# The last 256 tokens leave transposed and scaled on their way out of PSUM, and the end's products use both banks of a PSUM tile

## Chip, cores and metric

The kernel runs on one core of one Trainium2 chip. The metric is the device time of one execution in microseconds, given as the median of repeated runs. The two outermost times of the kernel before are 0.17% apart.

## The reference, cut to what matters

One layer of a streaming encoder is applied to 640 tokens (512 of a new prompt, 8 x 16 of running streams), with 1024 features each. Only its end is touched by the change: the down-projection of the ConvGLU, the residual, and the last RMSNorm.

```
D_MODEL = 1024
D_FF = ((8 * D_MODEL // 3 + 255) // 256) * 256        # 2816

def rms_norm(x, g):
    xf = x.astype(jnp.float32)
    y = xf * lax.rsqrt(jnp.mean(xf * xf, axis=-1, keepdims=True) + RMS_EPS)
    return (y * g.astype(jnp.float32)).astype(x.dtype)

def hybrid_layer(x, ...):
    ...
    out = h + (jax.nn.gelu(c) * b) @ p['w_down']
    return out, s_re, s_im, new_k, new_v, new_conv

y_prompt = rms_norm(hp, g_final)
y_sample = rms_norm(hs, g_final)
```

## The kernel before

Everything is kept transposed: features on the 128 partitions (8 blocks `h_[0..7]` of 128 features), the 640 tokens along the free axis. Every product with a weight is made of three products of split values (high x high, high x low, low x high), all through the helper `mm` (L115).

The order on each engine is written by hand. The program is a list of segments; `tick()` runs before each and issues what `later(n, fn)` has put down for that place. Each engine then works through its own queue in order, and waits on counters that the other engines advance.

The 2816 inner features go through the ConvGLU in six parts. The last part has `pn` = 4 blocks, and its down-projection is the end of the program. It goes over the tokens in two stretches, `segs = ((0, 384), (384, 640))`: first the eight output blocks i = 0..7 for tokens 0 to 383 (stretch A), then again the eight blocks for tokens 384 to 639 (stretch B). In the text "product i" is one such block: 4 inner blocks x 3 = 12 matmuls, issued by `fin_mm` in four calls, one per tick.

PSUM has two pools. `bigps()` gives a tile [128, 2, 512] of float32, which is two banks, from a ring of two such tiles (names `pb`). `smps(tag)` gives single banks `sX`, `sP`, `sS`, `sT`, one of each. `fin_mm` takes a fresh `bigps()` tile for each product and uses its bank 0 alone:

```
if k == 0:
    cur[i] = bigps()
ps = cur[i][:, 0, 0:e - a]
```

When a product is complete, `fin_evac` adds it to the residual (VectorE, L1505), squares it (ScalarE, L1509, L1511 or L1514), and adds the square to a running sum (VectorE, L1515). After product 7, `fin_stat` makes the RMSNorm scales: `s0` sums the squares over the partitions by matmuls with ones and takes the root (L1539 to L1541), `s1` refines the reciprocal on VectorE down to `ys`, one scale per token with tokens on partitions (L1544 to L1548), `s2` spreads it over all partitions by matmuls with the identity. For stretch A ScalarE copies that to `RS` (L1555), and the outputs follow during stretch B, two per product, by `fin_out`: one VectorE instruction h x gain x scale (L1524) and one DMA of SyncE (L1525). For stretch B the same eight VectorE instructions stand at the very end, reading the scale from PSUM, and their DMAs alternate between the queues of SyncE and ScalarE. The output `o_y` is (8, 128, 640), and the host turns it round.

Of the kernel before, what the change touches and what calls it, by code (L numbers as in the profile page):

```python
# [11 lines left out]
AF = mybir.ActivationFunctionType  # L12
OP = mybir.AluOpType
# [3 lines left out]
T, NS, TS = 640, 8, 16  # L17
HT = 320
D, DFF = 1024, 2816
KD, KF = 8, 22  # L20
# [5 lines left out]
SEG_A = 384  # L26
# [13 lines left out]
C_GM, C_GF, C_GO, C_CW, C_CB = 0, 8, 16, 24, 90  # L40
# [3 lines left out]
def body(nc, tc, d, ctx):  # L44
# [8 lines left out]
    V, A, G, PE, S = nc.vector, nc.scalar, nc.gpsimd, nc.tensor, nc.sync  # L53
# [3 lines left out]
    def nm(s):  # L57
        uid[0] += 1
        return f"{s}{uid[0]}"

    def ht(dt=F32, w=T):
        return heap.tile([128, w], dt, tag="T", name=nm("h"))

    def bigps():
        return psb.tile([128, 2, 512], F32, tag="big", name=nm("pb"))

    def smps(tag):
        return pss.tile([128, 512], F32, tag=tag, name=nm(tag))
# [4 lines left out]
    def vcol(c):  # L73
        return vec[:, c:c + 1]


    ident = const.tile([128, 128], F32, name="ident")
# [3 lines left out]
    RS = const.tile([128, T], F32, name="RS")  # L81
    rst = const.tile([128, 32], F32, name="rst")
# [31 lines left out]
    def mm(ps, lhs, rhs, start, stop):  # L114
        PE.matmul(ps, lhs, rhs, start=start, stop=stop)  # L115
# [19 lines left out]
    def later(n, fn):  # L135
        events.setdefault(clock[0] + n, []).append(fn)
# [3 lines left out]
    def tick():  # L140

        while clock[0] in events:
            for fn in events.pop(clock[0]):
                fn()
        if side[0] is not None:
            side[1] += side[2]
            while side[1] >= 1.0 and side[0] is not None:
                side[1] -= 1.0
                if next(side[0], "end") == "end":
                    side[0] = None  # L150
        clock[0] += 1
# [899 lines left out]
    n = 0  # L1051
# [32 lines left out]
    for i in range(8):  # L1084
        if i in (2, 4, 5, 6):
            p = pair()
            a = att[(2, 4, 5, 6).index(i)]
# [46 lines left out]
    a_t, c_t = tmp[:, 0:NA], tmp[:, NA:NA + L]  # L1134
# [112 lines left out]
    segs = []  # L1247
# [129 lines left out]
    def block(key, n):  # L1377
        c = 128 * (n % 4)
        return [t[:, c:c + 128] for t in ops[key][n // 4]]
# [45 lines left out]
    for p, nf in enumerate(PARTS):  # L1425
        for j in range(nf):
            f = f0 + j
            q = len(segs)
# [22 lines left out]
            e = q + 2 * (f == 0)  # L1451
# [7 lines left out]
            if prev is not None:  # L1459
# [8 lines left out]
                for o in range(per):  # L1468
                    i = j * per + o
# [11 lines left out]
    q = len(segs)  # L1481
# [16 lines left out]
    segs = ((0, SEG_A), (SEG_A, T))  # L1498
    accs = [ht(), ht()]
    last = [ht(), ht()]  # L1500

    def fin_evac(sg, i, ps):
        a, b = segs[sg]
        hs = h_[i][:, a:b]
        V.tensor_tensor(hs, ps, hs, op=OP.add)  # L1505

        def sq():
            if i == 0:
                A.activation(accs[sg][:, 0:b - a], hs, AF.Square)  # L1509
            elif i == 7:  # L1510
                A.activation(last[sg][:, 0:b - a], hs, AF.Square)  # L1511
            else:
                q = ht()
                A.activation(q[:, 0:b - a], hs, AF.Square)  # L1514
                V.tensor_tensor(accs[sg][:, 0:b - a], accs[sg][:, 0:b - a], q[:, 0:b - a], op=OP.add)  # L1515
        (later if sg == 0 else now)(1, sq)

    def now(n, fn):
        fn()

    def fin_out(sg, i, rs):
        a, b = segs[sg]
        o = ht()
        V.scalar_tensor_tensor(o[:, 0:b - a], h_[i][:, a:b], vcol(C_GO + i), rs, op0=OP.mult, op1=OP.mult)  # L1524
        (S if i % 2 == 0 or sg == 0 else nc.scalar).dma_start(d["o_y"][i, :, a:b], o[:, 0:b - a])  # L1525

    def fin_stat(sg):

        a, e = segs[sg]
        n, t0 = (e - a) // 128, a // 128  # L1530
        p1 = smps("sS")
        v, r, w = rst[:, 24:24 + n], rst[:, 16:16 + n], rst[:, 20:20 + n]
        y, ys = rst[:, 13:13 + n], rst[:, 27:27 + n]

        def s0():
            for t in range(n):
                for i, x in enumerate((accs[sg], last[sg])):
                    mm(p1[:, 2 * t:2 * t + 2], x[:, t * 128:t * 128 + 128], ones[:, 0:2], i == 0, i == 1)
            V.tensor_tensor(w, p1[:, 0:2 * n:2], rst[:, 8 + t0:8 + t0 + n], op=OP.mult)  # L1539
            A.activation(r, w, AF.Sqrt, scale=1.0 / D, bias=eps)  # L1540
            V.tensor_scalar(v, w, -0.5 / D, -0.5 * EPS, op0=OP.mult, op1=OP.add)  # L1541

        def s1():
            V.reciprocal(y, r)  # L1544
            V.tensor_tensor(r, y, y, op=OP.mult)
            V.tensor_tensor(r, r, v, op=OP.mult)
            V.scalar_tensor_tensor(y, r, 1.5, y, op0=OP.add, op1=OP.mult)
            V.tensor_tensor(ys, y, rst[:, t0:t0 + n], op=OP.mult)  # L1548

        def s2():  # L1550
            p2 = smps("sT" if sg == 0 else "sX")
            for t in range(n):
                mm(p2[:, t * 128:t * 128 + 128], rst[:, 27 + t:28 + t].to_broadcast([128, 128]), ident, True, True)
            if sg == 0:
                A.activation(RS[:, a:e], p2[:, 0:e - a], AF.Copy)  # L1555
            return p2
        return s0, s1, s2

    cur = {}

    def fin_mm(sg, b):
        i, k = divmod(b, pn)
        if k == 0:
            cur[i] = bigps()
        a, e = segs[sg]
        ps = cur[i][:, 0, 0:e - a]
        key, o = tail[i]
        hi, lo = block(key, o * pn + k)
        ch, cl = cs[pf + k]
        mm(ps, hi, ch[:, a:e], k == 0, False)  # L1570
        mm(ps, hi, cl[:, a:e], False, False)
        mm(ps, lo, ch[:, a:e], False, k == pn - 1)
        if k == pn - 1:
            later(0, lambda: fin_evac(sg, i, ps))
            if i == 7:
                st = fin_stat(sg)
                if sg == 0:
                    for j, f in enumerate(st):
                        later(4 + 2 * j, f)
                    for j in range(8):  # L1580
                        later(10 + 2 * j, lambda j=j: fin_out(0, j, RS[:, a:e]))
                else:
                    fin.extend(st)
    fin = []
    for b in range(8 * pn):
        tick()
        fin_mm(0, b)
    later(0, lambda: nc.scalar.dma_start(d["o_c"], oc))
    for b in range(8 * pn):
        tick()  # L1590
        fin_mm(1, b)
    tick()
    fin[0]()
    fin[1]()
    rs = fin[2]()[:, 0:T - SEG_A]
    for i in range(8):
        fin_out(1, i, rs)
    while events:
        tick()
    xctx2.close()  # L1600
# [84 lines left out]
    return o  # L1685


OUTS = {"o_y": (8, 128, T), "o_k": (4, 128, T), "o_v": (5, 128, 512), "o_s": (128, 2, 16, 9), "o_c": (128, KF, 18)}


def build(arrays):
    nc = bacc.Bacc("TRN2", target_bir_lowering=False, num_devices=1)
    d = {}
    for name, a in arrays.items():
        d[name] = nc.dram_tensor("in_" + name, a.shape, mybir.dt.from_np(a.dtype), kind="ExternalInput").ap()
    for name, s in OUTS.items():
        d[name] = nc.dram_tensor(name, s, F32, kind="ExternalOutput").ap()
    with tile.TileContext(nc) as tc, ExitStack() as ctx:
        body(nc, tc, d, ctx)
    return nc  # L1700


def unpack(r):
    y = r["o_y"].reshape(D, T).T
    k = r["o_k"].reshape(512, T).T
    v = r["o_v"].reshape(T, 512)
    s = r["o_s"].reshape(2, 64, 2, 16, 9).transpose(2, 4, 3, 0, 1).reshape(2, 9, 32, 64)
    cv = r["o_c"].transpose(2, 1, 0).reshape(18, DFF)

    def c(a, *shape):  # L1710
        return np.ascontiguousarray(a.reshape(shape))
    return (c(y[:512], 1, 512, D), c(y[512:], 8, 16, D),
            c(s[0, 0], 1, 1, 32, 64), c(s[1, 0], 1, 1, 32, 64),
            c(k[:512], 1, 1, 512, 8, 64), c(v[:512], 1, 1, 512, 8, 64),
            c(cv[:2], 1, 1, 2, DFF),
            c(s[0, 1:], 1, 8, 32, 64), c(s[1, 1:], 1, 8, 32, 64),
            c(k[512:], 1, 8, 16, 8, 64), c(v[512:], 1, 8, 16, 8, 64),
            c(cv[2:], 1, 8, 2, DFF))
# [7 lines left out]
```

## Time and profile before

| | |
|---|---|
| median of 3 runs | 951.29 us (951.09 to 952.75) |
| profiled execution, its own time | 955.98 us |
| its span, first to last instruction | 953.9 us |
| TensorE busy / VectorE / ScalarE / GpSimd | 97% / 66% / 46% / 14% of the span |
| mean granted TensorE clock | 0.985 of full speed |

The profile shows one execution, on one core. "PE" is TensorE's matmul, "PEld" its weight load, "DVE" VectorE, "ACT" ScalarE, "SP" SyncE; "PEq" or "SPq" is the instruction queue of an engine, from which DMAs are issued. A row of the timeline gives start, duration, engine, line, operation, what it writes and reads, and in brackets how long the engine had been idle and what ended that. Two matmuls in a row overlap in the records, so the distance of their starts is what one costs.

### The profile page before, as it was taken

To read this page: it belongs to the slowest core of one execution; us is meant where nothing else is said; L and a number is where in the kernel's file an instruction comes from. 1 tells how busy PE (TensorE), PEld (TensorE's weight loads), DVE (VectorE), ACT (ScalarE), POOL (GpSimd) and SP (SyncE) were. 2 spreads that over 40 slices of the span, in tenths; PEclk is the share of its full clock that TensorE was granted. 3 is DMA by queue.
4 is the path that set the end of the run, shared out by engine and by line. 5 is a ranking of instruction groups with operands and counts; after the bars stand their busy time and mean duration, and the time that the engine had idled before them with its cause. 6 is when DMAs were issued, how large, how long until landed. Compare 5 with 4: busy or idle time off the path is not lost.

```text
span 953.9 us, 16515 instructions
## 1 busy us (share of the span) xinstructions
PE 923.4 (97%) x6534; PEld 875.8 (92%) x6534; DVE 628.0 (66%) x1261; ACT 442.1 (46%) x689; POOL 133.4 (14%) x228
## 2 busy tenths in 40 slices
PE   8999999999999999999998989999999999999995
PEld 8978999977777799999998989999999999999994
DVE  6783996474665543566777877766766676666545
ACT  6244113343333364433667445545455545555441
POOL 0120403200000000000003212212122211222100
PEclk9999999999999999999999999999999999999998
DMA  6744329666647522234538778889878888899833
GB/s 223 198 137 125 133 68 110 216 199 215 169 129 230 159 81 67 72 105 158 136 84 178 156 165 188 206 186 200 196 178 187 201 191 180 197 191 192 189 57 110
DMA packets 62428, 151.76 MB, mean 159 GB/s; under 512 B 20944, under 2 KB 24208, under 8 KB 62352
## 3 DMA queue, kind: packets, MB, share of 16 engines
q1 hardware_dynamic: 45392, 95.90, 33.3%
q0 software_dynamic: 16096, 54.03, 29.9%
q8 instruction: 51, 0.84, 0.4%
q10 hardware_dynamic: 864, 0.78, 0.2%
q14 instruction: 25, 0.20, 0.1%
HBM read 114.56 MB, written 8.21 MB: 129 GB/s over the span
## 4 chain that ended last, share of the span: by engine, by line
PE 79%; DVE 7%; DMA 6%; ACT 4%; issue 2%; SPq 0%; DVEq 0%; ACTq 0%
PE pb L115 46%; PE sS L115 10%; PE sX L115 8%; PE sT L115 7%; PE sP L115 5%; DMA wl<-in_w 3%; DMA qs<-qs 2%; PE sT L738 1%; DMA fl<-s 1%; PE sX L814 1%; DVE h L1524 1%; DMA wr<-in_w 1%; DVE h L1198 1%; DVE tmp L1356 1%; PE sS L786 1%
## 5 line engine op out<-in xcount | busy, mean ns | idle before, releaser
L115 PE MATMUL pb<-h,wh 128*128 128x320 f32 (+2 forms) x2000 | 389.3, 316 | 4.9 <-ACT h L944 1.8
L115 PEld LDWEIGHTS pb<-h,wh 128*128 128x128 f32 x2000 | 314.2, 190 | 14.3 <-issue 6.6
L115 PE MATMUL pb<-h,wl 128*128 128x320 f32 (+2 forms) x1000 | 231.9, 311 | 0.4 <-DVE wl L112 0.4
L115 PEld LDWEIGHTS pb<-h,wl 128*128 128x128 f32 x1000 | 168.8, 189 | 0.9 <-DVE wl L112 0.7
L1288 POOL DMA_DIRECT2D fl<-s x41 | 35.7, 871 | 455.4 <-PE pb L115 271.8
L107 ACT ACTIVATE wh<-wr 128x1024 fp32r<-128x1024 f32 x50 | 52.7, 1054 | 82.0 <-PE pb L115 55.9
L112 DVE TENSOR_TENSOR wl<-wr,wh 128x1024 fp32r<-128x1024 f32 x50 | 61.1, 1221 | 39.5 <-ACT wh L107 39.3
L115 PE MATMUL sS<-h,wh 128*128 128x320 f32 x336 | 75.6, 312 | 0.0
L115 PE MATMUL sX<-h,fh 128*128 128x320 f32 x320 | 71.7, 312 | 0.0
L1286 ACT ACTIVATE fl<-s 128x1024 fp32r<-128x1024 f32 x41 | 43.3, 1057 | 56.3 <-PE sT L115 48.8
L693 ACT ACTIVATE sb<-sb,mx 128x128 f32<-128x128 f32 (+4 forms) x40 | 24.2, 605 | 73.7 <-DVE mx L692 49.0
L115 PEld LDWEIGHTS sS<-h,wh 128*128 128x128 f32 x336 | 57.0, 190 | 0.0
L115 PE MATMUL sS<-h,wl 128*128 128x320 f32 x168 | 53.0, 316 | 3.1 <-DMA wl<-in_w 3.1
L115 PEld LDWEIGHTS sX<-h,fh 128*128 128x128 f32 x320 | 54.2, 190 | 0.0
L1288 POOL DMA_DIRECT2D wl<-in_w x43 | 38.1, 887 | 87.0 <-ACT wl L1286 79.8
L115 PE MATMUL sX<-h,fl 128*128 128x320 f32 x160 | 49.8, 311 | 0.0
L1359 ACT ACTIVATE tmp<-tmp 128x512 f32<-128x512 f32 x22 | 13.9, 633 | 76.0 <-DVE tmp L1356 76.0
L1286 ACT ACTIVATE wl<-wr 128x1024 fp32r<-128x1024 f32 (+1 forms) x43 | 43.5, 1012 | 7.3 <-PE sS L115 6.2
L115 PE MATMUL sT<-h,gh 128*128 128x320 f32 x176 | 40.0, 315 | 4.5 <-DVE u L1445 4.5
L1287 ACT ACTIVATE wh<-wr 128x1024 fp32r<-128x1024 f32 (+1 forms) x43 | 43.1, 1003 | 0.0
L1287 ACT ACTIVATE fh<-s 128x1024 fp32r<-128x1024 f32 x41 | 42.9, 1046 | 0.0
L1356 DVE SCALAR_TENSOR_TENSOR tmp<-tmp,vec 128x656 f32<-128x656 f32 x44 | 39.5, 898 | 0.7
(338 smaller groups left out, 1684.2 us busy)
## 6 DMA issues: line engine op xcount, KB each, us to landing
wr<-in_w SPq DMA_DIRECT2D x112, 512.0 KB, 4.7
fl<-s POOLq DMA_DIRECT2D x41, 512.0 KB, 6.0
wl<-in_w POOLq DMA_DIRECT2D x39, 512.0 KB, 8.4
kc<-in_kc SPq DMA_DIRECT2D x16, 512.0 KB, 6.4
vc<-in_vc SPq DMA_DIRECT2D x16, 512.0 KB, 5.7
x<-in_x SPq DMA_DIRECT2D x7, 320.0 KB, 6.4
pb<-in_pbias SPq DMA_DIRECT2D x8, 256.0 KB, 7.4
h<-in_x SPq DMA_DIRECT2D x6, 320.0 KB, 4.5
```

The lines of the kernel that those rows point to most:

```text
L107: A.activation(hi, raws[u], AF.Copy)
L112: V.tensor_tensor(lo, raws[u], hi.bitcast(F32), op=OP.subtract)
L115: PE.matmul(ps, lhs, rhs, start=start, stop=stop)
L693: A.activation(sb[:, :w], sb[:, :w], AF.Exp, bias=mx[:, 2:3], accum_out=mx[:, 3:4])
L738: PE.transpose(pt[:, k * 128:k * 128 + 128], e[:, k * 128:k * 128 + 128], ident)
L786: PE.matmul(sc[32 * n:32 * n + 32, :], QB[:, hp, 4 * g4 + n].rearrange("p a b -> p (a b)"), kc[n // 2][:, n % 2, :], start=True, stop=True ...
L814: PE.matmul(sx[32 * n:32 * n + 32, 192:320], m["eT"][:, k * 128 + 32 * n:k * 128 + 32 * n + 32], vc[n // 2][:, n % 2, k, :], start=(k == 0 ...
L1286: A.activation(lo, src, AF.Copy, scale=-1.0)
L1287: A.activation(hi, src, AF.Copy)
L1288: G.dma_start(lo, src if again is None else again, accum_op=OP.add)
L1356: V.scalar_tensor_tensor(c_t, a_t[:, j:L + j], vcol(C_CW + 3 * f + j), c_t, op0=OP.mult, op1=OP.add)
L1359: A.activation(g_t[:, 0:512], c_t[:, 0:512], AF.Gelu_apprx_tanh)
```

## The change

Four things are changed, all in the end of the program.

1. `fin_mm` takes a `bigps()` tile for two products: product 2j uses bank 0, product 2j+1 bank 1 of the same tile.
2. In `fin_evac` the addition of the square goes to a later tick than the square. In stretch B the square comes at once, and ScalarE makes one more pass over the block: `hg` = h x gain (L1522), into space that the convolution no longer needs.
3. In stretch B each block `hg` is transposed by TensorE, 2 x (128 x 128), three ticks after its product (`flip`, L1535), so that the four single banks `sX`, `sP`, `sS`, `sT` fill up with 2 x 128 tokens on partitions and 1024 features along the free axis.
4. At the end of stretch B no scale is spread by matmuls. The four banks are evacuated with the scale of each token as a per-partition factor, two by VectorE and two by ScalarE (L1615, L1613), 128 x 512 each, and leave in four DMAs of 256 KB, on two queues, to a new output `o_z` (2, 128, 1024). The sums of squares of stretch B go to a `bigps()` tile, as `sS` is taken.

```diff
@@ fin_evac
+        q = accs[sg] if i == 0 else last[sg] if i == 7 else ht()
+
         def sq():
...
+            A.activation(q[:, 0:b - a], hs, AF.Square)
+
+        def add():
+            if 0 < i < 7:
                 V.tensor_tensor(accs[sg][:, 0:b - a], accs[sg][:, 0:b - a], q[:, 0:b - a], op=OP.add)
-        (later if sg == 0 else now)(1, sq)
...
+        if sg == 0:
+            later(1, sq)
+            later(2, add)
+        else:
+            sq()
+            later(2, add)
+            hg = gs[i % 2]
+            A.activation(hg, hs, AF.Copy, scale=vcol(C_GO + i))
+            if i < 7:
+                later(3, lambda: flip(i, hg))
+
+
+    gs = [a_t[:, 0:T - SEG_A], c_t[:, 0:T - SEG_A]]
+    TB = {}
+
+    def flip(i, hg):
+        for t in range(2):
+            key = (t, i // 4)
+            if key not in TB:
+                TB[key] = smps(("sX", "sP", "sS", "sT")[t + 2 * key[1]])
+            PE.transpose(TB[key][:, (i % 4) * 128:(i % 4) * 128 + 128], hg[:, t * 128:t * 128 + 128], ident)
...
-        p1 = smps("sS")
+        p1 = smps("sS") if sg == 0 else bigps()[:, 0]
...
@@ fin_mm
-        if k == 0:
-            cur[i] = bigps()
+        if k == 0 and i % 2 == 0:
+            cur[i // 2] = bigps()
         a, e = segs[sg]
-        ps = cur[i][:, 0, 0:e - a]
+        ps = cur[i // 2][:, i % 2, 0:e - a]
...
     fin[0]()
+    flip(7, gs[1])
     fin[1]()
-    rs = fin[2]()[:, 0:T - SEG_A]
-    for i in range(8):
-        fin_out(1, i, rs)
+    for n, (c, t) in enumerate(((0, 0), (0, 1), (1, 0), (1, 1))):
+        o = ht()[:, 0:512]
+        if n % 2:
+            A.activation(o, TB[t, c], AF.Copy, scale=rst[:, 27 + t:28 + t])
+        else:
+            V.tensor_scalar(o, TB[t, c], rst[:, 27 + t:28 + t], None, op0=OP.mult)
+        (S, nc.scalar)[n % 2].dma_start(d["o_z"][t, :, c * 512:c * 512 + 512], o)
...
-OUTS = {"o_y": (8, 128, T), "o_k": (4, 128, T), "o_v": (5, 128, 512), "o_s": (128, 2, 16, 9), "o_c": (128, KF, 18)}
+OUTS = {"o_y": (8, 128, SEG_A), "o_z": (2, 128, D), "o_k": (4, 128, T), "o_v": (5, 128, 512), "o_s": (128, 2, 16, 9), "o_c": (128, KF, 18)}
```

How the instructions stand on the engines is shown at three places. In brackets is the counter that an instruction waits for: DVE_49 is advanced by VectorE, Activation_49 by ScalarE, PE_49 by TensorE itself.

First TensorE in stretch A, from the end of product 0 to the start of product 3, before:

```order
L115 MATMUL pb_9581<-m_9539,wl_9448 128x384
L115 MATMUL pb_9600<-h_8935,wh_9447 128x384 [waits DVE_49]
...
L115 MATMUL pb_9600<-m_9539,wl_9448 128x384
L115 MATMUL pb_9615<-h_8935,fh_9461 128x384 [waits DVE_49]
...
L115 MATMUL pb_9632<-h_8935,fh_9461 128x384 [waits DVE_49]
```

and with the change:

```order
L115 MATMUL pb_9581<-m_9539,wl_9448 128x384
L115 MATMUL pb_9581<-h_8935,wh_9447 128x384 [waits DVE_49]
...
L115 MATMUL pb_9581<-m_9539,wl_9448 128x384
L115 MATMUL pb_9615<-h_8935,fh_9461 128x384 [waits PE_49]
...
L115 MATMUL pb_9615<-h_8935,fh_9461 128x384 [waits DVE_49]
```

Products 0 and 1 now write one tile, and so do 2 and 3. Before, each product waits for VectorE to have evacuated the tile that its ring slot held two products earlier: the count in the built program is that of product i-2's L1505 (for product 1, of the last L1396, the evacuation ahead of stretch A). With the change the even products carry no wait on VectorE, and the odd ones do: the count that product 1 waits for is the one that the L1505 of product 0 brings, for product 3 that of product 2, and so on through both stretches.

Second TensorE in stretch B, from the third quarter of product 4 to the start of product 5, before:

```order
L115 MATMUL pb_9817<-h_9339,fl_9529 128x256
L115 MATMUL pb_9817<-m_9539,fh_9528 128x256
L115 MATMUL pb_9817<-m_9540,fh_9528 128x256
L115 MATMUL pb_9817<-m_9539,fl_9529 128x256
L115 MATMUL pb_9840<-h_8935,fh_9528 128x256 [waits DVE_49]
```

and with the change:

```order
L115 MATMUL pb_9822<-h_9339,fl_9529 128x256
L1535 MATMUL sX_9755<-ident,tmp 128x128 [waits Activation_49]
L1535 MATMUL sP_9757<-ident,tmp 128x128
L115 MATMUL pb_9822<-m_9539,fh_9528 128x256
L115 MATMUL pb_9822<-m_9540,fh_9528 128x256
L115 MATMUL pb_9822<-m_9539,fl_9529 128x256
L115 MATMUL pb_9822<-h_8935,fh_9528 128x256 [waits DVE_49]
```

The two transposes of block 3 (`hg` is a part of `tmp`) stand between the ninth and the tenth matmul of product 4, and they wait for ScalarE's `hg` of block 3; the first matmul of product 5 waits for the evacuation of product 4.

Third VectorE in stretch B, from the evacuation of product 2 on, as a difference:

```order
 L1505 TENSOR_TENSOR h_5066<-pb_9771,h_5066 128x256
-L1515 TENSOR_TENSOR h_9577<-h_9577,h_9791 128x256
-L1524 SCALAR_TENSOR_TENSOR h_9801<-h_5066,vec,RS 128x384
-L1524 SCALAR_TENSOR_TENSOR h_9810<-h_5225,vec,RS 128x384
-L1505 TENSOR_TENSOR h_5225<-pb_9794,h_5225 128x256
...
+L1540 SCALAR_TENSOR_TENSOR h_9803<-h_5066,vec,RS 128x384
+L1514 TENSOR_TENSOR h_9577<-h_9577,h_9794 128x256
+L1540 SCALAR_TENSOR_TENSOR h_9815<-h_5225,vec,RS 128x384
+L1505 TENSOR_TENSOR h_5225<-pb_9771,h_5225 128x256
```

Before, the addition of the square stands right behind the evacuation and so waits for ScalarE; with the change an output of stretch A (L1540, before L1524) stands between them.

## Rows read from the trace of the kernel before

**Rows 1.** The page's chain of work that ended last, by engine.

```profile
PE 79%; DVE 7%; DMA 6%; ACT 4%; issue 2%; SPq 0%; DVEq 0%; ACTq 0%
```

**Rows 2.** Waits, 905 to 954 us: who waited for whom, total, times, longest.

```profile
PE pb L115 <- DVE h L1505: 1.8, 3, 0.6
```

**Rows 3.** Timeline, end of stretch A: start us, duration us, engine, line, operation.

```profile
925.91 0.34 PE L115 MATMUL pb<-m,wl 128*128 128x384 f32 x1
...
926.08 0.40 PE L115 MATMUL pb<-h,wh 128*128 128x256 f32 x2
...
926.28 0.56 DVE L1505 TENSOR_TENSOR h<-pb,h 128x384 f32<-128x384 f32 x1 [0.37 <-PE pb L115]
```

**Rows 4.** Timeline, products 0 to 2 of stretch B.

```profile
928.77 0.48 PE L115 MATMUL pb<-h,wh 128*128 128x256 f32 x2
...
929.22 0.42 DVE L1505 TENSOR_TENSOR h<-pb,h 128x256 f32<-128x256 f32 x1
...
929.67 0.42 ACT L1509 ACTIVATE h<-h 128x256 f32<-128x256 f32 x1 [0.23 <-DVE h L1505]
...
930.56 0.94 PE L115 MATMUL sT<-ident,rst 128*128 128x128 f32 x6
...
931.25 0.48 PE L115 MATMUL pb<-h,fh 128*128 128x256 f32 x2
...
931.53 0.49 ACT L1555 ACTIVATE RS<-sT 128x384 f32<-128x384 f32 x1 [1.44 <-PE sT L115]
```

**Rows 5.** Timeline, products 6 and 7 of stretch B.

```profile
938.35 0.42 DVE L1505 TENSOR_TENSOR h<-pb,h 128x256 f32<-128x256 f32 x1
...
938.83 0.51 PE L115 MATMUL pb<-h,wh 128*128 128x256 f32 x2 [0.61 <-DVE h L1505]
...
939.26 0.43 DVE L1515 TENSOR_TENSOR h<-h,h 128x256 f32<-128x256 f32 x1 [0.48 <-ACT h L1514]
...
939.60 1.14 DVE L1524 SCALAR_TENSOR_TENSOR h<-h,vec,RS 128x384 f32<-128x384 f32 x2
...
940.66 0.42 DVE L1505 TENSOR_TENSOR h<-pb,h 128x256 f32<-128x256 f32 x1
...
941.13 0.51 PE L115 MATMUL pb<-h,wh 128*128 128x256 f32 x2 [0.60 <-DVE h L1505]
```

**Rows 6.** Timeline, from the last matmul of product 7 to the end.

```profile
942.55 0.28 PE L115 MATMUL pb<-m,wl 128*128 128x256 f32 x1
...
943.15 0.42 DVE L1505 TENSOR_TENSOR h<-pb,h 128x256 f32<-128x256 f32 x1
...
946.24 0.16 DVE L1548 TENSOR_TENSOR rst<-rst 128x2 f32<-128x2 f32 x1
...
947.72 3.22 DVE L1524 SCALAR_TENSOR_TENSOR h<-h,vec,sX 128x256 f32<-128x256 f32 x8 [1.32 <-PE sX L115]
```

**Rows 7.** Timeline of TensorE, 196.5 to 197.9 us: transposes between matmuls of 320 columns.

```profile
196.97 0.38 PE L738 MATMUL sT<-ident,sb 128*128 128x128 f32 x2
197.10 0.83 PE L115 MATMUL pb<-h,wh 128*128 128x320 f32 x4
```

**Rows 8.** Groups by line and shape: out<-in, count | busy us, mean ns | idle before.

```profile
L689 DVE COPY eT<-sT 128x512 f32<-128x512 f32 x8 | 5.5, 687 | 3.9 <-PE sT L738 2.1 <-PE sT L802 1.8
...
L687 ACT ACTIVATE eT<-sT 128x512 f32<-128x512 f32 x8 | 4.7, 589 | 5.3 <-PE sT L802 4.3 <-PE sT L738 0.9
```

**Rows 9.** DMA, 945 to 956 us: GB/s in 40 slices; issues, KB each, us to landing.

```profile
GB/s 0 0 0 0 0 0 0 0 0 0 0 0 0 0 60 339 287 332 346 320 343 332 332 339 320 343 123 0 0 0 0 0 0 0 0 0 0 0 30 0
...
o_y<-h ACTq DMA_DIRECT2D x4, 128.0 KB, 1.7
```

**Rows 10.** DMA, 930 to 945 us, the same columns.

```profile
GB/s 0 0 0 0 0 0 0 0 0 0 0 287 369 360 33 0 0 266 344 385 53 0 0 209 340 377 123 0 0 147 365 369 168 0 0 0 0 0 0 0
...
o_y<-h SPq DMA_DIRECT2D x8, 192.0 KB, 1.9
```

**Rows 11.** Busy time by engine in stretches, PEclk granted TensorE clock (1.00 full).

```profile
946.00:947.00 1.00, 0.54 (x2) 0.54 (x3) 0.33 (x3) 0.00 (x0) 0.00 (x0) 0.63 0.00 0
```

More of the change, by code (lines that the diff above doesn't have):

```diff
@@ L1505, in fin_evac, with fin_out @@
         V.tensor_tensor(hs, ps, hs, op=OP.add)
+        q = accs[sg] if i == 0 else last[sg] if i == 7 else ht()
         def sq():
[L1508 to L1514, printed above, removed]
-                V.tensor_tensor(accs[sg][:, 0:b - a], accs[sg][:, 0:b - a], q[:, 0:b - a], op=OP.add)
-        (later if sg == 0 else now)(1, sq)
[L1518 to L1522, printed above, removed]
+            A.activation(q[:, 0:b - a], hs, AF.Square)
+        def add():
+            if 0 < i < 7:
+                V.tensor_tensor(accs[sg][:, 0:b - a], accs[sg][:, 0:b - a], q[:, 0:b - a], op=OP.add)
+        if sg == 0:
[16 more added lines that the diff above has]
+            PE.transpose(TB[key][:, (i % 4) * 128:(i % 4) * 128 + 128], hg[:, t * 128:t * 128 + 128], ident)
+    def fin_out(i, rs):
+        a, b = segs[0]
         o = ht()
         V.scalar_tensor_tensor(o[:, 0:b - a], h_[i][:, a:b], vcol(C_GO + i), rs, op0=OP.mult, op1=OP.mult)
-        (S if i % 2 == 0 or sg == 0 else nc.scalar).dma_start(d["o_y"][i, :, a:b], o[:, 0:b - a])
+        S.dma_start(d["o_y"][i], o[:, 0:b - a])
     def fin_stat(sg):
@@ L1550, in s2 @@
         def s2():
-            p2 = smps("sT" if sg == 0 else "sX")
+            p2 = smps("sT")
             for t in range(n):
                 mm(p2[:, t * 128:t * 128 + 128], rst[:, 27 + t:28 + t].to_broadcast([128, 128]), ident, True, True)
-            if sg == 0:
-                A.activation(RS[:, a:e], p2[:, 0:e - a], AF.Copy)
-            return p2
+            A.activation(RS[:, a:e], p2[:, 0:e - a], AF.Copy)
         return s0, s1, s2
@@ L1580, in fin_mm @@
                     for j in range(8):
-                        later(10 + 2 * j, lambda j=j: fin_out(0, j, RS[:, a:e]))
+                        later(10 + 2 * j, lambda j=j: fin_out(j, RS[:, a:e]))
                 else:
@@ L1703, in unpack @@
 def unpack(r):
-    y = r["o_y"].reshape(D, T).T
+    y = np.concatenate([r["o_y"].reshape(D, SEG_A).T, r["o_z"].reshape(T - SEG_A, D)], 0)
     k = r["o_k"].reshape(512, T).T
```

## The prediction

> **What bounds the kernel now.** The chain of work that ended last comes first: 79% of it is TensorE [rows 1], so a microsecond matters where TensorE stands still, or after its last matmul. The change touches only the last 45 us, so the next view is the waits of that stretch, and then the timeline, in four pieces. The waits show how little there is to win ahead of the last matmul: TensorE waits for evacuations three times there, 1.8 us in all [rows 2].
>
> Stretch A has no wait. The last matmul of a product and the first of the next are 0.17 us apart [rows 3], although the evacuation of the first begins 0.37 us after the start of that last matmul and takes 0.56: the next product writes another tile. Stretch B is slower. In its second half a product takes 941.13 - 938.83 = 2.30 us, where 12 matmuls of 256 columns need 12 x 0.12 = 1.44 (two together last 0.40, one 0.28, so one step is 0.12) [rows 3, 5, 6]. There VectorE sets the pace: evacuation, a wait for ScalarE's square, addition, two outputs, and 2.31 us from one evacuation to the next [rows 5]. After the last matmul, evacuation, sums, the scales and the eight outputs follow each other with nothing beside them [rows 6].
>
> **The change part by part.** Four prices come back. A waiting TensorE begins about 0.05 us after what it waits for (938.35 + 0.42 to 938.83 is 0.06), and its first two matmuls then take 0.51 in place of 0.40: 0.1 us to get going again [rows 3, 5]. An evacuation begins 0.03 us after the last matmul's end (925.91 + 0.34 to 926.28) [rows 3]. VectorE and ScalarE hand over 0.08 us before an instruction ends in the records, as in 939.26 + 0.43 to 939.60 [rows 5].
>
> *Two products in one tile, stretch A.* An odd product now waits for the evacuation of the even one before it, as the order on TensorE shows. Counted from the start of the even product's last matmul: its end at 0.34, evacuation 0.37 to 0.93, TensorE at 0.98, plus 0.1 to get going, against 0.17 before [rows 3]. That is 0.91 us, and products 1, 3, 5 and 7 pay it: **+3.6 us**. Behind the waiting matmul stands all of TensorE's queue, and nothing else has work to fill the gap. The even products find their banks long free. What bounds the price: without the 0.1 and with half the 0.05 it is 3.1, and 4.0 if the getting going costs double. The later tick of the addition does not change VectorE's order in stretch A and costs nothing; it lies in VectorE's idle time ahead of the next evacuation.
>
> *Stretch B.* Two costs are new, the same wait of odd products and the transposes. The trace has transposes of 128 x 128 between matmuls: two start 0.13 us apart from what follows, and the four matmuls after them take 0.83 where three steps of 0.15 and the 0.31 of the last would make 0.75 [rows 7]. I take 0.2 us for a pair. From both sides: 0.13, and twice 0.27 (the full record) if nothing overlaps.
>
> The Trainium skill, "TensorE: Matmul & The Clock Gate", section "Part 4: PE-mode transpose", gives about 275 ns for one in a kernel's context. The records agree with it [rows 7]; with that as the cost of each, the sum would be 2.4 us higher than mine.
>
> The stretch goes so, on the clock of the trace before:
> - Product 0 starts at 926.08. Product 1 waits for its evacuation, which stands behind the sums of stretch A and ends at 929.22 + 0.42 = 929.64; so it starts at 929.69 in place of 928.77 [rows 4]. It takes 0.1 + 1.44 + 0.2, `hg` of block 0 being ready in time (929.67 + 2 x 0.42). Then the matmuls that spread the scale of stretch A, 0.69 as before (930.56 to 931.25): product 2 starts at 932.12.
> - The transposes of block 1 wait for `hg`, which stands on ScalarE behind the copy to `RS`. That starts 0.97 after the spreading matmuls do, at 932.40, and then come 0.49 + 0.42 + 0.42 less two hand-overs [rows 4]: 933.57, TensorE at 933.62. With 0.1, the pair 0.2, two steps 0.24 and 0.28, product 2 ends at 934.44, and product 3 starts after the evacuation, at 934.44 + 0.03 + 0.42 + 0.05 = 934.94. It takes 1.74; product 4 starts at 936.68.
> - From here on a pair repeats. An even product starts 0.16 us before its predecessor's end; then evacuation, square and `hg` (0.03 + 0.42, 0.03 + 0.34 + 0.42) and the wake-up bring the transposes to 1.45 after its start, where nine matmuls need 1.08. Its end is at 1.45 + 0.1 + 0.2 + 0.24 + 0.28 = 2.27, the odd one starts at 2.77 and takes 1.74: 4.51 us a pair, against 4.60 before. So product 6 starts at 941.19, product 7 at 943.96, and ends 1.90 later, at 945.86.
>
> Before it ends at 942.55 + 0.28 = 942.83 [rows 6]: **+3.0 us**. What VectorE won by not waiting for squares is lost to two waits of TensorE. VectorE is no longer the pace: 0.35 + 0.34 + 1.06 = 1.75 us of work for each product [rows 5]. Bounds: +1.8 with transposes at 0.13 and no getting going, +5.4 with transposes at 0.54 a pair.
>
> *After the last matmul.* The evacuation of product 7 stood behind an addition and began 0.32 us after the end; now 0.03: **-0.3**. From there to the scales nothing changes, and the last scale is ready at 946.24 + 0.16 = 946.40 before [rows 6]. The extra pass of ScalarE and the last transposes lie beside the small VectorE steps.
>
> *The outputs.* Before, 1.32 us of spreading matmuls and 3.22 us of outputs follow, up to 950.94; the last DMA is issued then and lands 1.7 us later, 6.27 us after the scale [rows 6, 9]. Now an evacuation of 128 x 512 follows at once: no such one with a factor from PSUM is in the trace, the nearest are copies, 0.69 us on VectorE and 0.59 on ScalarE [rows 8]; two outputs of 256 columns take 0.81 [rows 6], the upper bound; the choice hardly matters, because the DMAs end later. A DMA of 128 KB lands in 1.7 us and one of 192 KB in 1.9 [rows 9, 10]; 128 KB at the 385 GB/s seen at best are 0.34, which leaves 1.36 of fixed time. All four together are 1.05 MB, and move at 337 to 385 GB/s [rows 9, 10], in 2.7 to 3.1 us. So the last lands about 0.65 + 1.36 + 2.9 = 4.9 us after the scale: **-1.4 us**. Bounds: -1.1 at the lower rate, and -2.5 if the rate is no limit (last issue at 1.6, landing 2.1).
>
> **Sum:** 3.6 + 3.0 - 0.3 - 1.4 = +4.9 us. The profiled execution took 955.98 us, 4.7 above the median 951.29; it would take 960.9, and the median 951.29 + 4.9 = **956.2 us**, 0.5% slower. A measurement of this kernel tells about 0.2%, 1.9 us, from no change.
>
> **The rivals.** (1) The two banks give room, not slower: an odd product starts while the even one is being evacuated. Stretch A then costs nothing. In stretch B only the transposes hold TensorE, 1.45 + 0.1 + 0.2 + 0.36 = 2.11 a product: product 3 starts at about 933.5, product 7 four products later, at 941.9, and ends at 944.2: +1.4, and the sum is +1.4 - 0.3 - 1.4 = -0.3, 951.0 us. For it: the banks are different, and in the trace before evacuation and next product do run side by side [rows 3]. Against it: the count in the built program, which leaves TensorE no choice. The point from which it decides is whether TensorE starts product 1 of stretch A before the evacuation of product 0 has ended. Chance 0.07.
>
> The Trainium skill, "Perfetto Trace Analysis", section "Matmuls", has matmul groups rotate through different banks so that one's evacuation overlaps the next one's matmuls. By that rule rival 1 would be the outcome; the trace before shows it for separate tiles [rows 3], and no run here yet for two banks of one tile.
>
> (2) The clock falls. The new gaps could bring TensorE to the lower of its two levels, 1.2 GHz, in stretch B: 96 steps of 0.12 us would take 0.11 more each, +10.5 us, of which some 1.5 hide in the waits; 965 us. For it: the clock does fall in the trace before, once TensorE has stood still after the sums [rows 11]. Against it: 0.6 us of waiting in each 2.3 us did not bring it down earlier; the new gaps are 0.9 in 5 us and twice some 0.5 in 4.5. Chance 0.04.
>
> (3) The end gives more: the DMAs are not bound by their rate, and getting going costs nothing. Then 3.1 + 1.8 - 0.3 - 2.5 = +2.1, 953.4 us, at the edge of what can be told. Chance 0.04.
>
> **How the numbers follow.** Forecast 0.85, rivals 0.07, 0.04, 0.04. The range goes from the sum of the lower bounds, which is rival 3, to the forecast with the transposes at their upper bound (+2.4): 953.4 to 958.6; rivals 1 and 2 are left out. Faster 0.03 (rival 1 with a better end), same 0.08 (the rest of rival 1, half of rival 3), slower 0.89.
>
> **What would show it.** In stretch A, four waits of TensorE for L1505, each idle some 0.5 to 0.8 us in the records, and the products in pairs of about 5.1 us in place of 4.2. In stretch B, waits for L1522 in the even products and for L1505 ahead of the odd ones, 4.5 us a pair. Four transfers of 256 KB that run together, and no TensorE work after the last transposes. Wrong I would be, if product 1 of stretch A starts without a gap, if the granted clock falls before the sums, or if the transfers of the end take much less than 2.7 us.

## The result and the profile after

The changed kernel takes 957.68 us (median of 4 runs, 955.73 to 957.96), the kernel before, timed beside it, 952.02: ratio 1.0064, 95% interval 1.0045 to 1.0082. It is 5.7 us slower, where 4.9 had been forecast. The profiled execution took 957.79 us with a span of 956.0.

Stretches that run from the first matmul of stretch A to the end of the span are compared best, because what lies ahead of them differs from execution to execution (the end began at 909.36 us in the execution shown of before, at 904.54 in this one). A is from the first matmul of 384 columns of product 0 to the first of 256, B from there to the end of the last matmul of product 7, then to the end of the instruction that makes the scales, then to the end of the span.

| us | A | B | to the scales | outputs | A to the end |
|---|---|---|---|---|---|
| before | 16.72 | 16.75 | 3.57 | 7.50 | 44.54 |
| after | 20.49 | 21.32 | 3.30 | 6.35 | 51.46 |
| change | +3.77 | +4.57 | -0.27 | -1.15 | +6.92 |
| forecast | +3.6 | +3.0 | -0.3 | -1.4 | +4.9 |

The two profiled executions are 6.9 us apart in this stretch, the medians 5.7; the interval of the ratio, 4.3 to 7.8 us, holds both.

The waits of the changed kernel, 904 to 956 us, answer to [rows 2], where TensorE waited three times for 1.8 us:

```profile
PEld pb L115 <- DVE h L1505: 6.9, 8, 1.0
PE pb L115 <- DVE h L1505: 4.9, 8, 0.8
...
PE sS L1535 <- ACT tmp L1522: 0.3, 1, 0.3
PE sX L1535 <- ACT tmp L1522: 0.3, 1, 0.3
```

Eight waits for evacuations are the eight odd products, four in each stretch. In stretch A one looks so (timeline of TensorE and VectorE, products 0 and 1), to be held against [rows 3]:

```profile
906.55 0.34 PE L115 MATMUL pb<-m,wl 128*128 128x384 f32 x1
...
906.92 0.56 DVE L1505 TENSOR_TENSOR h<-pb,h 128x384 f32<-128x384 f32 x1 [1.80 <-PE pb L115]
...
907.54 0.62 PE L115 MATMUL pb<-h,wh 128*128 128x384 f32 x2 [0.65 <-DVE h L1505]
```

From the start of the last matmul of product 0 to the first of product 1 it is 907.54 - 906.55 = 0.99 us, where two products were 0.17 apart before. The other bank of the tile is not in use all that time.

Stretch B begins as follows (TensorE, products 0 to 2; `sS` are the sums of stretch A, L1535 the transposes, `sT` the spreading of the scale):

```profile
926.46 1.40 PE L115 MATMUL sS<-ones,h 128*128 128x2 f32 x12
928.64 0.51 PE L115 MATMUL pb<-h,wh 128*128 128x256 f32 x2 [0.78 <-DVE h L1505]
...
929.48 0.63 PE L115 MATMUL pb<-h,wh 128*128 128x256 f32 x2
...
930.12 0.41 PE L1535 MATMUL sX<-ident,tmp 128*128 128x128 f32 x1
...
930.98 0.41 PE L115 MATMUL pb<-m,wl 128*128 128x256 f32 x1
931.19 1.48 PE L115 MATMUL sT<-ident,rst 128*128 128x128 f32 x6
```

Two matmuls of 256 columns take 0.63 us here and not 0.40, one 0.41 and not 0.28. The busy time by engine in stretches of one us shows why (after the engines' columns PEclk, the granted clock):

```profile
928.00:929.00 1.00, 0.36 (x3) 0.36 (x4) 0.90 (x6) 0.68 (x3) 0.00 (x0) 1.00 0.00 0
929.00:930.00 1.00, 1.00 (x9) 1.00 (x8) 0.38 (x3) 0.43 (x2) 0.00 (x0) 0.71 0.00 0
930.00:931.00 1.00, 1.00 (x7) 1.00 (x7) 0.00 (x0) 0.00 (x0) 0.00 (x0) 0.50 0.06 16
931.00:932.00 1.00, 1.00 (x6) 1.00 (x6) 0.42 (x1) 0.00 (x0) 0.00 (x0) 0.50 0.00 0
932.00:933.00 1.00, 1.00 (x8) 1.00 (x7) 0.00 (x0) 0.29 (x1) 0.00 (x0) 0.59 0.00 0
933.00:934.00 1.00, 0.91 (x9) 0.70 (x7) 0.77 (x2) 0.90 (x3) 0.00 (x0) 1.00 0.00 0
```

For 3.4 us, from about 929.4 to 932.8, the granted clock is at 0.50, the lower level of 1.2 GHz (a slice of 0.71 is 0.58 us of it, one of 0.59 is 0.82). Ahead of it TensorE did the twelve 128x2 sums and then waited for the evacuation of product 0. Later the pairs are steady (TensorE, products 4 to 6):

```profile
937.01 0.40 PE L115 MATMUL pb<-h,fh 128*128 128x256 f32 x2
938.54 0.33 PE L1535 MATMUL sX<-ident,tmp 128*128 128x128 f32 x1 [0.29 <-ACT tmp L1522]
...
939.85 0.50 PE L115 MATMUL pb<-h,fh 128*128 128x256 f32 x2 [0.52 <-DVE h L1505]
...
941.60 0.40 PE L115 MATMUL pb<-h,wh 128*128 128x256 f32 x2
```

A pair takes 941.60 - 937.01 = 4.59 us: the even product waits for ScalarE's `hg` ahead of its transposes, the odd one for VectorE ahead of its first matmul.

The end answers to [rows 6, 8, 9] (VectorE, ScalarE and the DMA issues; then the transfers, 945 to 956 us, GB/s in 40 slices):

```profile
949.49 0.16 DVE L1564 TENSOR_TENSOR rst<-rst 128x2 f32<-128x2 f32 x1
949.68 0.69 ACT L1613 ACTIVATE h<-sP,rst 128x512 f32<-128x512 f32 x1 [1.02 <-DVE rst L1564]
949.68 0.75 DVE L1615 TENSOR_SCALAR h<-sX,rst 128x512 f32<-128x512 f32 x1
...
951.09 0.69 ACT L1613 ACTIVATE h<-sT,rst 128x512 f32<-128x512 f32 x1 [0.71 <-ACT h L1613]
951.80 0.34 ACTq L1616 DMA_DIRECT2D o_z<-h  x1
```
```profile
GB/s 0 0 0 0 0 0 0 0 0 0 0 0 0 0 0 0 0 0 0 0 0 0 60 380 395 365 380 373 417 365 358 395 313 22 22 0 0 0 0 0
...
o_z<-h ACTq DMA_DIRECT2D x2, 256.0 KB, 3.0
o_z<-h SPq DMA_DIRECT2D x2, 256.0 KB, 3.2
```

Nine full slices of 0.275 us and two in part: the megabyte moves in some 2.8 us, at 358 to 417 GB/s. Behind it follow two slices at 22 GB/s, to which the account of the outputs comes back.

### The profile page after: what moved, and what is told of

Same layout as the page of the kernel before. It is cut to its first block, busy times and chain, and to the rows that moved or that the text cites. A ratio compares the mean times of both kernels' runs of the same rounds, so it can differ in the third digit from the quotient of the medians.

```text
span 956.0 us, 16538 instructions
## 1 busy us (share of the span) xinstructions
PE 923.0 (97%) x6546; PEld 873.9 (91%) x6546; DVE 626.2 (66%) x1255; ACT 446.5 (47%) x699; POOL 133.2 (14%) x228
## 4 chain that ended last, share of the span: by engine, by line
PE 80%; DVE 7%; DMA 5%; ACT 5%; issue 2%; SPq 1%; ACTq 0%; DVEq 0%
PE pb L115 46%; PE sS L115 10%; PE sX L115 8%; PE sT L115 7%; PE sP L115 5%; DMA wl<-in_w 3%; DMA qs<-qs 2%; DMA wr<-in_w 1%; PE sT L738 1%; PE sX L814 1%; DVE h L1198 1%; DVE tmp L1356 1%; DVE h L1505 1%; PE sS L786 1%; ACT wh L107 1%
```

## The experiments

Each run was timed beside the kernel before on the same chip, and has one profiled execution, from which its stretches are taken. The table has the stretches of every run; the text tells them apart. The ratio is the one on record, not the quotient of the two medians beside it: in run 8 the medians are only 2.1 us, 0.22%, apart.

| | A | B | to the scales | outputs | A to the end | median us (before) | ratio, 95% interval |
|---|---|---|---|---|---|---|---|
| 1 tile for each product | 16.74 | 18.80 | 3.30 | 6.33 | 45.17 | 952.16 (951.15) | 1.0020, 1.0002 to 1.0038 |
| 2 shared tile alone | 20.48 | 19.94 | 3.32 | 6.97 | 50.71 | 957.06 (951.15) | 1.0062, 1.0042 to 1.0082 |
| 3 one-bank tiles | 16.75 | 18.80 | 3.30 | 6.32 | 45.17 | 955.16 (951.15) | 1.0034, 1.0011 to 1.0058 |
| 4 transposes later | 20.47 | 19.51 | 3.30 | 5.86 | 49.14 | 956.32 (951.15) | 1.0050, 1.0032 to 1.0068 |
| 5 sums later | 20.49 | 21.46 | 3.30 | 6.32 | 51.57 | 959.62 (951.77) | 1.0074, 1.0049 to 1.0099 |
| 6 shared in B only | 16.73 | 21.07 | 3.30 | 6.36 | 47.46 | 953.96 (950.75) | 1.0038, 1.0023 to 1.0053 |
| 7 shared in A only | 20.46 | 18.81 | 3.30 | 6.37 | 48.94 | 956.24 (950.75) | 1.0053, 1.0036 to 1.0070 |
| 8 own tiles, transposes later | 16.72 | 15.88 | 3.31 | 5.84 | 41.75 | 949.63 (951.77) | 0.9958, 0.9939 to 0.9977 |
| 9 the same, DMAs from SyncE | 16.72 | 15.90 | 3.30 | 5.90 | 41.82 | 948.39 (951.77) | 0.9965, 0.9944 to 0.9985 |
| 10 one-bank tiles, transposes later | 16.74 | 15.89 | 3.31 | 5.85 | 41.79 | 949.80 (951.77) | 0.9980, 0.9958 to 1.0001 |

**1. A tile for each product**, in the changed kernel:

```
-        if k == 0 and i % 2 == 0:
-            cur[i // 2] = bigps()
+        if k == 0:
+            cur[i] = bigps()
-        ps = cur[i // 2][:, i % 2, 0:e - a]
+        ps = cur[i][:, 0, 0:e - a]
```

> The changed kernel with its one-product-per-tile allocation back: each product again takes a tile of its own, bank 0, while the transposed exit stays. Theory (the shared tile makes the odd product wait): stretch A is back at some 16.7 us from 20.5, the clock stays at its higher level after the sums, stretch B ends about 1.4 us later than before, since only the transposes hold TensorE, and the outputs keep their gain of 1.1 to 1.4 us; in all within 1 us of the kernel before. Rival (the transposes and ScalarE's extra pass are what costs): still 4 to 6 us slower than before.

Stretch A is 16.74 us, as before the change. Every wait for L1505 in a product is gone, the granted clock stays at 1.00 to the end of TensorE's work, and stretch B is 18.80. Without the shared tile the new way out costs 2.05 us net there, where 1.4 had been expected. The median is 1.0 us above that of the kernel before, and the rival is out. TensorE's waits, 907 to 946 us:

```profile
PE sS L1535 <- ACT tmp L1522: 0.9, 3, 0.3
PE pb L115 <- ACT h L1510: 0.8, 1, 0.8
PE sX L1535 <- ACT tmp L1522: 0.8, 3, 0.3
...
PE sX L1535 <- issue: 0.5, 1, 0.5
```

Six of the transposes wait for `hg` (L1522). The 0.8 of L1510 is the sums at the end, and the last row is a gap of 0.5 us ahead of the first transposes that the profile puts down to no wait. The shared tile thus cost 51.46 - 45.17 = 6.3 us, of which 3.75 in stretch A.

**2. The shared tile alone**, in the kernel before (the same four lines the other way round):

> The kernel before with the tile for two products alone, outputs as before. Theory (shared tile): stretch A 3.7 us longer, four waits of TensorE in it; stretch B 1.5 us longer, and up to 1.3 more if the clock falls after the sums as it did in the changed kernel; in all 5 to 6.5 us slower. Rival (the exit costs, not the tile): no slower than before, or faster by what the three bank waits of stretch B took, 1.8 us.

It loses the same 6 us without any transpose, and the granted clock falls here too, to 0.50 from 926.0 to 929.4 us. Stretch B is 3.19 us longer, a little over the 2.8 that were expected at most. All of that lies in its first half: products 4 to 7 take 8.42 us (933.19 to 941.61) and took 8.60 before (934.23 to 942.83), where they already waited for evacuations [rows 5].

**3. Four tiles of one bank**, in the changed kernel:

```
+    pse = pctx.enter_context(tc.tile_pool(name="pse", bufs=4, space=PSUM))
...
+    def onebank():
+        return pse.tile([128, 512], F32, tag="one", name=nm("pb"))
...
+            cur[i] = onebank()
+        ps = cur[i][:, 0:e - a]
```

> The changed kernel, its end with four tiles of one bank each in place of two tiles of two banks: the same four banks in the same turn, but each product a tile of its own. Theory (the wait belongs to the tile, not to the bank): TensorE has no waits in stretch A, apart from some 0.7 us once where the PSUM pools change over; stretch B as in the run with bank 0 alone; 0 to 1.5 us slower than before. Rival (neighbouring banks hold each other up, whoever owns them): as slow as the changed kernel, 5 to 6 us.

The stretches equal those of run 1 to 0.01 us, with one-bank tiles in place of two-bank ones that are half empty. What waits goes with the tile, and neighbouring banks do not hold each other up: the rival is out. The time misses its forecast all the same, 4.0 us above the kernel before by the medians and not 0 to 1.5. The two pools of PSUM are closed and opened anew ahead of the end, so the first matmul of stretch A waits 1.53 us for the evacuation before it, in place of 0.79. That is 0.7 of the 3 us by which the median lies above run 1. The rest stays open; run 10, with the same pools, shows no such distance to run 8.

**4. Transposes one tick later**, in the changed kernel:

```
-                later(3, lambda: flip(i, hg))
+                later(4, lambda: flip(i, hg))
```

> The changed kernel with each block's transposes one tick later, between two products in place of ahead of a product's last quarter, so that ScalarE's block is ready and part of the wait for the evacuation is filled. Theory (in stretch B the even products lose some 0.4 us each to the wait for ScalarE, on top of the tile's wait): pairs of 3.9 us in place of 4.5, 1.7 us less than the changed kernel in all. Rival (transposes cost by themselves, wherever they stand): pairs as before, no change against the changed kernel.

The waits for L1522 are gone, and a pair takes 939.77 - 935.78 = 3.99 us in place of 4.59 (TensorE):

```profile
935.78 0.51 PE L115 MATMUL pb<-h,fh 128*128 128x256 f32 x2 [0.55 <-DVE h L1505]
...
939.77 0.51 PE L115 MATMUL pb<-h,fh 128*128 128x256 f32 x2 [0.41 <-DVE h L1505]
```

Stretch B is 1.8 us shorter, although the clock fell in it as well (0.50 from 930 to 933 us). The medians tell less of it: 5.2 us above the kernel before, for 5.7 with the change, and the two intervals overlap.

**5. The sums of stretch A one tick later**, in the changed kernel:

```
-                        later(4 + 2 * j, f)
+                        later(5 + 2 * j, f)
```

> The changed kernel with the sums of stretch A one block later: the twelve 128x2 matmuls stand inside product 1 and no longer right ahead of its wait for the evacuation. Stretch A stays at 20.5 us by either theory. Theory 1 (the clock fell because the slim matmuls and the wait of 0.78 us stood back to back): the granted clock stays at 1.00 at the start of stretch B, stretch B is 20.0 us in place of 21.3, the time 1.3 us below that of the changed kernel. Theory 2 (the 1.4 us of slim matmuls alone bring it down): the clock falls all the same, about where they stand, and stretch B stays at 21 to 21.5 us.

The clock falls all the same, which was the second theory's forecast, but the run doesn't decide: the wait is still beside the sums, now ahead of them instead of behind (TensorE, and one stretch of the clock).

```profile
928.82 0.50 PE L115 MATMUL pb<-h,wh 128*128 128x256 f32 x2 [0.52 <-DVE h L1505]
...
929.27 1.40 PE L115 MATMUL sS<-ones,h 128*128 128x2 f32 x12
```
```profile
932.00:934.00 2.00, 2.00 (x11) 2.00 (x10) 0.60 (x3) 0.57 (x2) 0.00 (x0) 0.50 0.00 0
```

In run 1 the same sums run with no wait beside them and the clock stays, so the sums alone are not the cause. The next two runs take the waits of the two stretches apart.

**6. The shared tile in stretch B alone:**

```
+        if k == 0 and (i % 2 == 0 or sg == 0):
+            cur[i if sg == 0 else i // 2] = bigps()
...
+        ps = cur[i][:, 0, 0:e - a] if sg == 0 else cur[i // 2][:, i % 2, 0:e - a]
```

> The changed kernel with a PSUM tile for each product in stretch A, and the shared tile in stretch B alone: prices the B term without the A term. Stretch A 16.7 us. Theory 1 (the clock falls only where the four waits of stretch A have gone before the slim sums): granted clock 1.00 throughout, stretch B 20.0 us (21.3 less the 1.3 of the clock), start of A to the end 46.4 us, 1.9 above the kernel before. Rival (the sums with the wait of 0.78 us behind them are enough): clock 0.50 for some 3 us at the start of stretch B, stretch B 21.3, 47.7 us in all.

Stretch A is free of waits, and the clock falls as in the changed kernel: the rival holds. TensorE, and then the stretches:

```profile
921.99 1.40 PE L115 MATMUL sS<-ones,h 128*128 128x2 f32 x12
924.17 0.51 PE L115 MATMUL pb<-h,wh 128*128 128x256 f32 x2 [0.78 <-DVE h L1505]
```
```profile
924.00:925.00 1.00, 0.83 (x7) 0.83 (x8) 0.85 (x6) 0.82 (x2) 0.00 (x0) 1.00 0.00 0
925.00:926.00 1.00, 1.00 (x8) 1.00 (x7) 0.00 (x0) 0.00 (x0) 0.00 (x0) 0.62 0.00 0
926.00:927.00 1.00, 1.00 (x7) 1.00 (x6) 0.27 (x1) 0.00 (x0) 0.00 (x0) 0.50 0.06 16
```

**7. The shared tile in stretch A alone** (the same lines with `sg == 1`):

> The opposite: the shared tile in stretch A alone, a tile for each product in stretch B. Stretch A 20.5 us. Theory 1 (the waits of stretch A and the slim sums bring the clock down, no wait behind them is needed): clock 0.50 soon after the sums, stretch B 18.8 and 1.3 for the clock, 20.1 us, 50.2 us from the start of A to the end. Rival (the wait of 0.78 us in stretch B is part of the cause): clock 1.00 throughout, stretch B 18.8, 48.9 us in all.

Here stretch A has its four waits of 0.65 us, the sums follow, no wait stands beside them, and the clock stays at 1.00: the rival again. Stretch B is that of run 1. TensorE, and the stretches:

```profile
929.45 1.40 PE L115 MATMUL sS<-ones,h 128*128 128x2 f32 x12
930.71 0.48 PE L115 MATMUL pb<-h,wh 128*128 128x256 f32 x2
```
```profile
930.00:931.00 1.00, 1.00 (x10) 1.00 (x10) 0.11 (x1) 0.64 (x1) 0.00 (x0) 1.00 0.00 0
931.00:932.00 1.00, 1.00 (x9) 0.82 (x7) 0.90 (x6) 0.69 (x3) 0.00 (x0) 1.00 0.00 0
932.00:933.00 1.00, 0.50 (x5) 0.51 (x5) 0.37 (x3) 0.43 (x2) 0.00 (x0) 1.00 0.00 0
```

**8. A tile for each product, and transposes one tick later** (the edits of runs 1 and 4 together):

> The changed kernel with a PSUM tile for each product and the transposes one block later: both waits that the change added are gone. Theory 1 (these two waits are the whole loss, and the new way out of the chip is a gain): stretch A 16.7 us, stretch B 18.8 less 7 waits of 0.29, so 16.6 to 16.9 us, no clock fall, and with 3.3 to the scale and 6.3 for the outputs 43.0 to 43.3 us in all against 44.5 of the kernel before: 1.3 us faster, ratio 0.9986. Rival (the work that came to ScalarE and VectorE is the next bound in stretch B): stretch B stays near 18.5 us and the time within 0.3 us of the kernel before.

It beats both kernels: 0.42% below the one before by the ratio (interval 0.23 to 0.61%), with a stretch 2.8 us shorter. Up to the last matmul of product 7 no wait of TensorE's matmuls is left but the first, for L1396. The rival falls: VectorE and ScalarE keep up.

Stretch B is 15.88 us, 0.7 less than the least expected. The forecast gave back the idle 0.29 of each wait, but a product takes 1.78 in place of 2.16 (931.35 to 933.13 us here, 931.77 to 933.93 in run 1), 0.38 less; the gap of 0.5 us ahead of the first transposes is gone too. TensorE in run 1, then here, the last matmul ahead of a transpose and the transpose:

```profile
933.17 0.28 PE L115 MATMUL pb<-h,fl 128*128 128x256 f32 x1
...
933.74 0.33 PE L1535 MATMUL sX<-ident,tmp 128*128 128x128 f32 x1 [0.29 <-ACT tmp L1522]
```
```profile
932.74 0.28 PE L115 MATMUL pb<-m,fl 128*128 128x256 f32 x1
...
932.94 0.33 PE L1535 MATMUL sX<-ident,tmp 128*128 128x128 f32 x1
```

From the one start to the other it is 0.57 us with the wait and 0.20 without. The profile counts idle time from the end of the matmul's record, 0.28 us behind its start; without a wait the transpose starts ahead of that end. What comes behind is the same in both: the next matmul starts 0.19 us after the transpose.

**9. The same with all four DMAs issued by SyncE:**

```
-        (S, nc.scalar)[n % 2].dma_start(d["o_z"]...
+        S.dma_start(d["o_z"]...
```

> The run with a tile for each product and later transposes, and all four output DMAs issued by SyncE, so that ScalarE's second 128x512 copy doesn't stand behind the issue of its first DMA (0.71 us). Theory 1 (the last copy's time sets the end): the last copy is ready 0.4 to 0.7 us earlier and the outputs take 5.7 us in place of 6.3. Rival (1 MB at 370 to 410 GB/s is 2.6 to 2.8 us whatever comes first): the outputs stay at 6.2 to 6.4 us, the time equal to that of the other run.

ScalarE's second copy ends 1.30 us behind the scales in place of 1.85 (940.02 + 0.68 less 939.40; 942.82 + 0.69 less 941.66), and the outputs are as long as before, 5.90 us. An earlier copy thus gains nothing here. That what has to move sets the end, the rival's core, is argued and not shown by this run alone: with one queue the last issue comes later, 2.21 us behind the scales (941.61) in place of 1.87 (943.53). For it speaks that in both runs the data move without a pause, from 1.6 to 4.5 us behind the scales. The interval of the ratio overlaps that of run 8.

**10. One-bank tiles and later transposes** (runs 3 and 4 together):

> Four tiles of one bank each for the products of the end, and the transposes one block later. Theory 1 (the wait belongs to the tile, and what the run with four one-bank tiles lost came from the change-over of the pools ahead of the end): the stretches of the end as in the run with own two-bank tiles and later transposes, 43.0 to 43.3 us from the start of stretch A, and the time 1 to 3 us above that run's. Rival (there is no cost ahead of the end and that run's time was scatter): the same time as with own two-bank tiles, about 949.8 us where the kernel before takes 951.1.

The stretches are those of run 8, and the median lies 0.2 us from it: the rival holds, the change of pools has no cost that can be told. The interval of the ratio just reaches no change against the kernel before.

## Why the prediction was right, and where it was off

**Stretch A, right.** Forecast 0.91 us for each of four odd products, measured 0.99 + 0.11 (two matmuls in 0.62 and not 0.51) - 0.17 = 0.93. The evacuation began 0.37 us behind the start of the last matmul, as in [rows 3]. Runs 1, 3 and 6, where stretch A has a tile for each product, and runs 2 and 7, where it shares them, show that the price belongs to the shared tile and to nothing else. The rule of the Trainium skill, "Perfetto Trace Analysis", section "Matmuls", that groups rotate through banks so that evacuation and matmuls overlap, holds here for separate tiles (runs 1 and 3, no gap). For two banks of one tile it brought nothing, as the program itself carries the wait: rival 1 is out.

**Stretch B, mis-sized: +4.57 for +3.0.** Product 1 starts 928.64 - 925.03 = 3.61 us behind the start of the stretch, exactly the forecast (929.69 - 926.08). From there to product 2 it is 932.33 - 928.64 = 3.69 us in place of 2.43: 1.26 us more, in matmuls at the lower clock (the spreading of the scale alone takes 1.14 us from start to start, 931.19 to 932.33, for 0.69 in [rows 4]). From product 2 to the end it is 14.02 for 13.74, the pairs 4.59 for 4.51. So the step that failed is rival 2: the working weighed the clock by the length and spacing of the gaps ("0.9 in 5 us and twice some 0.5 in 4.5") and gave it 0.04, for the whole stretch. It didn't look at what stands directly ahead of a gap. The twelve sums, in the kernel before between two full products, now have a wait of 0.78 us behind them. Rival 2 came true in a short form: 3.4 us at half clock, 1.26 us lost and not 9. The sign named for it, the granted clock falling before the sums of the end, did show. Runs 6 and 7 take the causes apart: with the wait beside the sums the clock falls in stretch B whatever stretch A did (the changed kernel, runs 2, 4, 5 and 6), and in no profile does it fall there without it (the kernel before, runs 1, 3 and 7 to 10). A wait without the sums did not do it either: the first matmul of stretch A waits 0.79 us for an evacuation, in run 3 1.53 us, and the clock stays at 1.00. Why the two together bring it down stays open.

That the time still lies in the range is in part luck. The room above the forecast was kept for transposes at their upper bound (+2.4), and it was the clock that used it.

**The transposes, right in kind.** In the changed kernel the even products from 4 on wait for `hg`; the transposes start 1.53 us after the product (937.01 to 938.54), 1.45 had been reckoned. In run 1 all products from 2 on wait, 0.22 to 0.29 us. A pair of them costs 0.21 us where nothing waits (product of run 8 from 927.85 to 929.50, 1.65 for 1.44) and up to 0.34 (1.78); 0.2 was taken. The 0.27 us of one record, which [rows 7] with its pairs does not show, is the median of this row of the kernel before (least, median and longest in ns):

```profile
L738 PE MATMUL sT<-ident,sb x80: 269/273/422, 192.1 to 329.1; 128*128 128x128 f32 x80
```

The 275 ns of the Trainium skill ("TensorE: Matmul & The Clock Gate", section "Part 4: PE-mode transpose") agree with that record. It is not what one transpose adds to the stream.

**After the last matmul, right**: -0.27 for -0.3.

**The outputs, nearly: -1.15 for -1.4.** The four transfers do run at their common rate for 2.8 us. (The lower rate of 337 GB/s stands in none of [rows 9, 10]; the full slices of [rows 9] average 330, which is 0.07 us on the sum.) ScalarE's copy took 0.69 us, and its second waited 0.71 behind the first; in run 9, where it doesn't wait, the outputs are no shorter than in run 8. Two things beside the change are in this number.

Some 0.5 us of it belong to the clock. In the kernel before the scale is spread at the lower clock [rows 11], and VectorE waits 1.32 us for it [rows 6]. Run 2 has the same end, spreads the scale at a granted clock of 1.00, and has outputs of 6.97 us:

```profile
944.98 0.71 PE L115 MATMUL sX<-ident,rst 128*128 128x128 f32 x4 [1.57 <-DVE rst L1548]
945.73 3.22 DVE L1524 SCALAR_TENSOR_TENSOR h<-h,vec,sX 128x256 f32<-128x256 f32 x8 [0.80 <-PE sX L115]
```

Against that the new way out is 0.62 us shorter.

The other thing is half a microsecond by which the changed kernel's own outputs differ: they last 5.84 to 5.90 us in the four runs with later transposes, and 6.32 to 6.37 in the changed kernel and the five other runs with its end. It goes with a packet of 8 KB of the instruction queue. In those six this packet moves 3.25 to 3.57 us behind the scales, among the output's rows, and the last rows follow alone, at some 22 GB/s, until 4.95 to 4.97. In the four others it moves before the output, and the last row ends at 4.51 to 4.54. No run moves the packet by itself, so this is a likely cause and not a shown one.

## What to carry to other kernels

A buffer shared by two products binds the second to the release of the first, even where they write different banks, because the program counts its waits per tile; look at what the order makes wait, and give each product a tile of its own. A new step in a busy engine's queue is cheap if it is issued a tick after its input is ready: issued too early, the new way out costs 2.05 us in stretch B, and a tick later the stretch is 0.87 us shorter than in the kernel before. When a wait of TensorE is priced, look at what it did beside the wait as well as at the length.

## What the runs showed of the hardware

- TensorE's granted clock went to 0.50 for 3.4 us (changed kernel) after 1.4 us of 128x2 matmuls with a wait of 0.78 us behind them, or with one of 0.52 us ahead of them (run 5). Neither the sums without a wait beside them (runs 1 and 7), nor four waits of 0.65 us between full products (stretch A), nor one of 1.53 us (run 3, ahead of stretch A) did that. Against the forecast it cost 1.26 us. The clock also falls ahead of 570 us in every profile; what stands beside those falls stays open.
- The Trainium skill, "TensorE: Matmul & The Clock Gate", section "Loop structure matters more than you think", says that a copy out of PSUM doesn't break the warmth of the engine, in a loop whose next matmuls follow at once. Here the next matmuls waited for the copy: four times in stretch A that left the clock alone, and beside the sums it did not.
- 128 x 512 from PSUM with a scale per partition took 0.75 us on VectorE and 0.69 on ScalarE, against 0.69 and 0.59 for plain copies [rows 8].
- A product whose transposes waited 0.29 us by the records lost 0.38 (2.16 us in run 1, 1.78 in run 8), since without a wait the transpose starts before the record of the matmul ahead of it ends.
